# One query tile of two heads in place of two query tiles of one head, in a sparse attention job

## The chip, the cores and the metric

One Trainium2 chip, one of its eight cores. The metric is the device time of one execution in microseconds (us), the median of several runs. A difference of about 0.5% (11 us) is what a measurement of this kernel can tell from no change.

The engines that matter: TensorE multiplies (PE in the profile; PEld is its load of the stationary operand, of which there is one for every matmul), VectorE (DVE) and ScalarE (ACT) do elementwise work, GpSimd (POOL) and SyncE (SP) mostly issue DMAs. In this kernel TensorE's results go to PSUM tiles, which DVE and ACT read.

## The reference

Two layers over a sequence of 1024 tokens. Each has one input projection, two token mixers that read it (stick-breaking attention, 8 heads; native sparse attention, 8 heads in 2 groups of 4, the heads of a group sharing keys and values), gates, two projections that are merged, and an output projection. The sparse part, which is what changes, per query position and head (head size 64):

```
o_cmp: softmax over compressed blocks (up to 63), values vc
sel  : the 8 blocks of 64 keys with the largest group-summed o_cmp probability (some forced)
o_slc: softmax over the keys of the selected blocks, causal,  values vs
o_win: softmax over the last 256 keys,                        values vw
out  = g0 * o_cmp + g1 * o_slc + g2 * o_win        g = sigmoid(gate_logits), per head
b    = out * silu(n_z)
```

All four heads of a group use the same `kc, vc, ks, vs, kw, vw`.

## The kernel before

Everything is f32 in and out. Matmuls run on f32r operands, each value split into a high and a low part: ACT casts the high part out of PSUM, DVE subtracts it to get the low part (`split`, L136 and L137). A product of activations and weights takes three matmuls (L194, L196, L198), an attention product with values two (L917 with the high part, L918 with the low part, in `av`).

A layer runs in stages: `early` (projections for keys, values, queries, gates), `nsa` (sparse attention), `sb` (stick-breaking attention), `output`. In `nsa` and `sb` the attention is cut into jobs, and the rest of the projections is the fill between: `run_jobs` interleaves the scores of the next job (list A) with the products of the current one (list B), and after each step `pump` issues projection matmuls worth a share of the job's planned time (`nsa_us`, four numbers by sequence position m, for four jobs each per group). The framework's scheduler may then move an instruction whose inputs are ready; the order shown further down is the final one.

Before, a sparse job (`head_job`) is one head h over 256 queries: query tiles x = 0 and 1, that is tiles i = 2m and 2m+1 of 128 queries. Scores of tile i span (i+1) x 128 selected keys and min(i+1, 3) x 128 window keys (`nsa_scores`). The exponentials E and ew are scaled by 1/sum and the gate (`nsa_scale`), then turned to keys-by-queries by 128x128 transposes on TensorE (L898), up to four of them in a PSUM tile `tr` (a stage of the `pipeline`, three `tr` buffers), split into `wh` and `wl`, and multiplied with V (`av`). A key tile that both query tiles see gives a matmul of 256 columns. The last key tile is seen by x = 1 alone, and the first of the window by x = 0 alone: those matmuls have 128 columns (`av_stages`, `nsa_av`). The result has the products with V's high part on rows 0 to 63 and low part on 64 to 127; `merge` (L935 on ACT, L936 on DVE) adds them, into the upper or lower half of a 128-row tile by the head's parity, and after two heads `finish_pair` loads the SiLU gate `szl` and multiplies (L926, 128x256).

Of the kernel before, what the change touches and what calls it, by code (L numbers as in the profile page):

```python
# [10 lines left out]
F32 = mybir.dt.float32  # L11
# [4 lines left out]
ALU = mybir.AluOpType  # L16
# [4 lines left out]
P = 128  # L21
S = 1024
# [65 lines left out]
class Trunk:  # L88
    def __init__(self, tc, I, O, depth=2, dbg=None):
        self.tc, self.nc, self.I, self.O, self.depth = tc, tc.nc, I, O, depth  # L90
        self.dbg = dbg or {}
        self.n = 0
        self.fill = []
        self.debt = 0.0
        self.clock, self.seq, self.later = 0.0, 0, []
        self.plan, self.at, self.loaded = [], 0, {}

        self.nsa_us = (1.97, 4.16, 5.85, 7.05)
        self.sb_us = (1.34, 2.87, 4.77, 6.04)
# [12 lines left out]
        self.scb = 2  # L112
        self.adb = 5
# [873 lines left out]
    def nsa(self, l):  # L987
        tc, nc = self.tc, self.nc
        with tc.tile_pool(name=f"nsa{l}", bufs=2, reuse_waits="tile") as pool:
# [9 lines left out]

            def head_job(n, h, st):  # L1000
                g, m = n // 4, n % 4
                hs = {}
                A, B = [], []
                if h == 0:
                    A.append(lambda: load_q(n + 1))
                if m == 3 and h == 3:
                    A.append(lambda: load_kv(g + 1) if g == 0 else self.sb_first())
                for x in range(2):
                    A += self.nsa_scores(pool, g, m, h, x, lambda: qs[n], lambda: kv[g], cmp[n], hs)
                B.append(lambda: self.nsa_scale(pool, g, m, h, hs, cmp[n]))  # L1010
                B += self.nsa_av(pool, g, m, h, lambda: kv[g], cmp[n], hs)

                def fin():
                    if h % 2 == 0:
                        st["o"] = self.tl(pool, [P, 256], F32, "o")
                    self.merge(pool, hs["ps"], st["o"], h % 2)
                    if h % 2 == 1:
                        hd = g * 4 + h - 1
                        self.finish_pair(pool, st["o"], 512 + hd * 64, m, hd * 64)
                B.append(fin)  # L1020
                return A, B, self.nsa_us[m]

            jobs = [cmp_job(0)]
            for n in range(8):
                st = {}
                for h in range(4):
                    if h == 2 and n + 1 < 8:
                        jobs.append(cmp_job(n + 1))
                    jobs.append(head_job(n, h, st))
            self.run_jobs(jobs)  # L1030

    def nsa_cmp(self, pool, g, m, x, q, st):

        nc = self.nc
# [17 lines left out]
        if i == 0:  # L1052
            nc.vector.tensor_tensor(s, s, self.cst("v_cmp").unsqueeze(1).to_broadcast([P, 4, 8]), ALU.mult)
        pg = self.tl(pool, [P, 4, 64], F32, "cpg")
        if nn < 64:
            nc.vector.memset(pg[:, :, nn:64], 0.0)
        gates = self.G[:, i, g * 4:g * 4 + 4]
        if i >= 4:
            nc.vector.tensor_tensor(s, s, rs.unsqueeze(2).to_broadcast([P, 4, nn]), ALU.mult)
            st["sel"][x] = self.nsa_select(pool, i, s, nn)  # L1060
            nc.vector.tensor_tensor(pg[:, :, 0:nn], s, gates.unsqueeze(2).to_broadcast([P, 4, nn]), ALU.mult)
        else:
            gr = self.tl(pool, [P, 4], F32, "cgr")
# [33 lines left out]

    def nsa_scores(self, pool, g, m, h, x, q, kv, cm, hs):

# [7 lines left out]
        def begin():  # L1107
            hs["e", x] = self.tl(pool, [P, S], F32, "E", bufs=4)
            hs["w", x] = self.tl(pool, [P, 384], F32, "ew", bufs=4)
            hs["mx", x] = self.tl(pool, [P, 3], F32, "mx", bufs=4)  # L1110
            if x == 0:
                hs["rs"] = self.tl(pool, [P, 2, 2], F32, "rs")
            return q()[:, h, x * P:x * P + P]

        def row():
            qt = begin()
            ps = self.scores(qt, kv()[0], 0, nk, [])
            nc.vector.tensor_tensor_reduce(hs["e", x][:, 0:nk], ps, self.cst("b_mask")[:, 640 - nk:640], -1.0, 3e38,
                                           ALU.add, ALU.min, hs["mx", x][:, 1:2])

        def half(c):
            qt = begin() if c == 0 else q()[:, h, x * P:x * P + P]
            c1 = min(nk, c * 512 + 512)
            b = c1 - c * 512
            mx = hs["mx", x]
            ps = self.scores(qt, kv()[0], c * 512, c1, [(i * P, "m_causal")] if c == 1 else [])
            bias = cm["sel"][x][:, c * 8:c * 8 + b // 64].unsqueeze(2).to_broadcast([P, b // 64, 64])
            nc.vector.tensor_tensor_reduce(  # L1128
                hs["e", x][:, c * 512:c1].rearrange("p (a b) -> p a b", b=64),
                ps.rearrange("p (a b) -> p a b", b=64), bias, -1.0,  # L1130
                3e38 if c == 0 else mx[:, 0:1], ALU.add, ALU.min, mx[:, c:c + 1])

        def win():
            e, ew, mx, rs = hs["e", x], hs["w", x], hs["mx", x], hs["rs"]
            ps = self.scores(q()[:, h, x * P:x * P + P], kv()[1], k0, nk, [])
# [4 lines left out]
            nc.scalar.activation(e[:, 0:nk], e[:, 0:nk], AF.Exp, bias=mx[:, 1:2], scale=-1.0,  # L1140
                                 accum_out=rs[:, 0, x:x + 1])
            nc.scalar.activation(ew[:, 0:n], ew[:, 0:n], AF.Exp, bias=mx[:, 2:3], scale=-1.0,
                                 accum_out=rs[:, 1, x:x + 1])

        return ([row] if i < 4 else [lambda: half(0), lambda: half(1)]) + [win]

    def nsa_scale(self, pool, g, m, h, hs, cm):

        nc = self.nc
        f = self.tl(pool, [P, 2, 2], F32, "f")  # L1150
        nc.vector.reciprocal(f, hs["rs"])
        gates = self.G[:, 2 * m:2 * m + 2, :].rearrange("p i (b h) -> p b i h", h=8)[:, 1:3, :, g * 4 + h]
        nc.vector.tensor_tensor(f, f, gates, ALU.mult)
        for x in range(2):
            nk = (2 * m + x + 1) * P
            n = min(nk, 384)
            e, ew = hs["e", x], hs["w", x]
            nc.vector.tensor_scalar(e[:, 0:nk], e[:, 0:nk], f[:, 0, x:x + 1], None, ALU.mult)
            nc.scalar.mul(ew[:, 0:n], ew[:, 0:n], f[:, 1, x:x + 1])
        hs["ps"] = self.tl(self.pav, [P, 512], F32, "av", bufs=1)  # L1160

    def nsa_cmp_av(self, g, h, hs, cm):

        c = (h // 2) * 256
        self.av(hs["ps"], [(self.VCS[:, g, h % 2, :], cm["ch"], cm["cl"], (c, c + 256), (0, 256))], False, False)

    def nsa_av(self, pool, g, m, h, kv, cm, hs):
        stages = self.av_stages(pool, m, lambda: (hs["e", 0], hs["e", 1]), lambda: kv()[2])

        def wb(kt, x):  # L1170
            i = 2 * m + x
            k0 = max(0, i - 2)
            return hs["w", x][:, (kt - k0) * P:(kt - k0) * P + P]

        if m > 0:
            a = 2 * m
            stages.append((lambda: [wb(a - 1, 0), wb(a - 1, 1), wb(a, 0), wb(a, 1)],
                           lambda: [(kv()[3][:, a - 1, :], (0, 256), (0, 256)), (kv()[3][:, a, :], (256, 512), (0, 256))]))
            stages.append((lambda: [wb(a - 2, 0), wb(a + 1, 1)],
                           lambda: [(kv()[3][:, a - 2, :], (0, 128), (0, 128)),  # L1180
                                    (kv()[3][:, a + 1, :], (128, 256), (128, 256))]))
        else:
            stages.append((lambda: [wb(0, 0), wb(0, 1), wb(1, 1)],
                           lambda: [(kv()[3][:, 0, :], (0, 256), (0, 256)), (kv()[3][:, 1, :], (256, 384), (128, 256))]))
# [306 lines left out]
```

## Time and profile before

| what | value |
|---|---|
| median of 3 runs | 2206.55 us (2206.5 to 2213.57) |
| the profiled execution | 2207.63 us, its span 2205.8 us (1.8 us lie around it) |
| busy: PE, PEld, DVE, ACT, POOL | 96%, 83%, 72%, 51%, 3% of the span |
| granted TensorE clock, mean over the span | 0.993 |
| `nsa`, layer 0 and 1 | about 297 to 686 us and 1367 to 1757 us |
| `sb`, layer 0 and 1 | about 686 to 954 us and 1757 to 2023 us |

A busy share of PE counts each matmul from its start to its modelled end, and matmuls overlap. How much of the engine one takes is read from start to start in the timeline, not from its duration.

### The profile page before, as it was taken

The numbers are of one execution on the slowest core, as the hardware profiler recorded it, in microseconds if no ns is written. First come the engines' busy times: TensorE is split into PE (matmuls) and PEld (weight loads), VectorE is DVE, ScalarE is ACT, GpSimd is POOL, SyncE is SP. The second block draws the span as 40 slices with busy tenths as digits, with TensorE's granted clock in tenths as the row PEclk, the third lists the DMA queues.
The fourth block names the chain that finished last, engine by engine and source line by source line (L and its number), as shares of the span: only waits on it lengthen the run. The fifth ranks groups of instructions, "written<-read, shape, count | busy, mean of one in ns | idle before, by whom it ended". The sixth has DMA issues, their size and how long they took to land.

```text
span 2205.8 us, 36824 instructions
## 1 busy us (share of the span) xinstructions
PE 2113.4 (96%) x13128; PEld 1831.2 (83%) x13128; DVE 1578.4 (72%) x3722; ACT 1131.5 (51%) x2489; POOL 73.0 (3%) x242
## 2 busy tenths in 40 slices
PE   3999999999999999999999999999999999999999
PEld 3899788988988777779899988889898877777899
DVE  5758568878867778786866863887787587787643
ACT  4433146556666656663533422665666566556410
POOL 2200000000000000000010000000000000001000
PEclk8999999999999999999999999999999999999999
DMA  7546922243225455176456473222522443534433
GB/s 290 108 139 193 303 93 82 91 139 107 78 62 148 125 139 125 64 253 189 151 165 168 129 206 121 92 90 74 149 92 78 124 125 105 148 101 165 152 123 103
DMA packets 254104, 297.05 MB, mean 135 GB/s; under 512 B 38888, under 2 KB 201568, under 8 KB 253920
## 3 DMA queue, kind: packets, MB, share of 16 engines
q1 hardware_dynamic: 213152, 250.65, 37.4%
q10 hardware_dynamic: 36224, 29.37, 5.1%
q0 software_dynamic: 4544, 14.68, 2.4%
q8 instruction: 103, 1.69, 0.3%
q14 instruction: 81, 0.66, 0.1%
HBM read 206.28 MB, written 83.89 MB: 132 GB/s over the span
## 4 chain that ended last, share of the span: by engine, by line
PE 70%; DVE 17%; DMA 5%; issue 3%; ACT 3%; POOL 1%; SPq 1%; DVEq 0%; ACTq 0%; POOLq 0%
PE proj L194 16%; PE proj L198 16%; PE proj L196 16%; PE tr L898 6%; DVE C L1281 4%; PE av L918 4%; PE av L917 3%; PE sc L885 3%; PE sc L886 3%; DVE E L1282 3%; DVE wl L137 2%; DVE w L137 2%; DMA actlo<-AD 1%; DMA ada<-in_ada_w 1%; PE tr L436 1%
## 5 line engine op out<-in xcount | busy, mean ns | idle before, releaser
L194 PE MATMUL proj<-acthi,w 128*128 128x512 f32 x1312 | 537.6, 410 | 3.8 <-ACT acthi L136 1.4
L198 PE MATMUL proj<-acthi,w 128*128 128x512 f32 x1312 | 538.8, 411 | 0.0
L196 PE MATMUL proj<-actlo,w 128*128 128x512 f32 x1312 | 535.1, 408 | 0.5 <-DVE actlo L137 0.5
L136 ACT CAST w<-raw 128x512 fp32r<-128x512 f32 (+1 forms) x296 | 183.2, 622 | 224.0 <-PE proj L198 136.8
L137 DVE TENSOR_TENSOR wl<-tr,wh 128x512 fp32r<-128x512 f32 (+2 forms) x432 | 257.7, 611 | 48.8 <-ACT wh L136 46.1
L194 PEld LDWEIGHTS proj<-acthi,w 128*128 128x128 f32 x1312 | 249.0, 190 | 42.2 <-ACT acthi L136 2.3
L196 PEld LDWEIGHTS proj<-actlo,w 128*128 128x128 f32 x1312 | 248.8, 190 | 36.7 <-DVE actlo L137 1.9
L198 PEld LDWEIGHTS proj<-acthi,w 128*128 128x128 f32 x1312 | 248.5, 189 | 33.9
L137 DVE TENSOR_TENSOR w<-raw,w 128x512 fp32r<-128x512 f32 (+1 forms) x296 | 202.8, 689 | 87.5 <-ACT w L136 84.0
L136 ACT CAST wh<-tr 128x512 fp32r<-128x512 f32 (+2 forms) x432 | 223.0, 527 | 79.9 <-PE tr L898 74.1
L194 PE MATMUL proj<-w,acthi 128*128 128x256 f32 (+1 forms) x768 | 222.3, 290 | 6.8 <-ACT G L813 3.4
L918 PE MATMUL av<-wl,V 128*128 128x256 f32 (+1 forms) x864 | 217.0, 284 | 6.5 <-DVE wl L137 6.5
L198 PE MATMUL proj<-w,actlo 128*128 128x256 f32 (+1 forms) x768 | 221.7, 289 | 0.0
L196 PE MATMUL proj<-w,acthi 128*128 128x256 f32 (+1 forms) x768 | 220.5, 287 | 0.0
L917 PE MATMUL av<-wh,V 128*128 128x256 f32 (+1 forms) x864 | 214.7, 269 | 0.3
L898 PE MATMUL tr<-ident,E 128*128 128x128 f32 x1152 | 187.7, 275 | 22.9 <-DVE E L1282 22.0
L898 PEld LDWEIGHTS tr<-ident,E 128*128 128x128 f32 x1152 | 140.4, 140 | 67.9 <-DVE E L1282 35.2
L1281 DVE TENSOR_TENSOR_SCAN C<-C 128x128 f32<-128x128 f32 (+7 forms) x128 | 173.1, 1352 | 30.7 <-ACT C L1277 29.9
L918 PEld LDWEIGHTS av<-wl,V 128*128 128x128 f32 x864 | 162.7, 188 | 30.1 <-DVE wl L137 17.8
L885 PE MATMUL sc<-kk,q 128*128 128x512 f32 (+3 forms) x512 | 174.4, 341 | 8.0 <-DVE mx L1128 4.3
L886 PE MATMUL sc<-kk,q 128*128 128x512 f32 (+3 forms) x512 | 175.7, 343 | 0.0
L917 PEld LDWEIGHTS av<-wh,V 128*128 128x128 f32 x864 | 163.0, 189 | 10.5 <-ACT wh L136 1.5
(247 smaller groups left out, 3900.1 us busy)
## 6 DMA issues: line engine op xcount, KB each, us to landing
raw<-in_w_in SPq DMA_DIRECT2D x168, 256.0 KB, 3.1
ada<-in_ada_w SPq DMA_DIRECT2D x48, 512.0 KB, 5.5
kk<-QK SPq DMA_DIRECT2D x48, 512.0 KB, 7.4
q<-QK ACTq DMA_DIRECT2D x64, 256.0 KB, 3.9
QK<-s SPq DMA_DIRECT2D x32, 512.0 KB, 2.9
MD<-sz SPq DMA_DIRECT2D x64, 256.0 KB, 2.5
QK<-s SPq DMA_DIRECT2D x48, 256.0 KB, 4.1
VD<-s SPq DMA_DIRECT2D x48, 256.0 KB, 2.0
```

Source lines behind the costliest of these rows:

```text
L136: nc.scalar.copy(hi, src)
L137: nc.vector.tensor_tensor(lo, src, hi.bitcast(F32), ALU.subtract)
L194: nc.tensor.matmul(ps, lh, rh, start=(x == 0), stop=False)
L196: nc.tensor.matmul(ps, lh, rl, start=False, stop=False)
L198: nc.tensor.matmul(ps, ll, rh, start=False, stop=(x == n - 1))
L885: nc.tensor.matmul(ps, q, k[:, 0, c0:c1], start=True, stop=False)
L886: nc.tensor.matmul(ps, q, k[:, 1, c0:c1], start=False, stop=not masks)
L898: nc.tensor.transpose(pt[:, x * P:x * P + P], b, self.ident)
L917: nc.tensor.matmul(ps[:, c:d], lhsT, hi[:, a:b], start=(first and x == 0), stop=False, skip_group_check=True)
L918: nc.tensor.matmul(ps[:, c:d], lhsT, lo[:, a:b], start=False, stop=(last and x == n - 1), skip_group_check=True)
L1281: nc.vector.tensor_tensor_scan(rev, rev, rev, 1.0, ALU.mult, ALU.bypass)
L1282: nc.vector.tensor_tensor(e[:, 0:nk], e[:, 0:nk], c[:, 1:nk + 1], ALU.mult)
```

## The change

A job is now one query tile of 128 queries for two heads of a group (`pair_job`, heads 2hp and 2hp+1 as r = 0, 1). Both heads see the same key tiles, so every product with V has 256 columns: 128 queries of head r = 0, then those of r = 1. A stage is two (key tile, branch) units, four transposes; an odd last unit makes a stage of two. The compressed probabilities are laid out so that the heads of a pair stand side by side too. `merge` and `finish_pair` are replaced by `nsa_merge` and `nsa_finish`: the output tile has 64 rows with the two heads side by side, [64, 2, 256], and the gate load, the multiplication and the store take that shape. `nsa_us` gets eight numbers, one for each tile. The memory set aside for DMA descriptors of GpSimd's queue goes to 8192 bytes.

```
-        self.nsa_us = (1.97, 4.16, 5.85, 7.05)
+        self.nsa_us = (1.5, 2.4, 3.85, 4.5, 5.6, 6.1, 6.85, 7.3)
...
-            def head_job(n, h, st):
+            def pair_job(n, hp, x, st):
...
-                for x in range(2):
-                    A += self.nsa_scores(pool, g, m, h, x, lambda: qs[n], lambda: kv[g], cmp[n], hs)
-                B.append(lambda: self.nsa_scale(pool, g, m, h, hs, cmp[n]))
-                B += self.nsa_av(pool, g, m, h, lambda: kv[g], cmp[n], hs)
+                for r in range(2):
+                    A += self.nsa_scores(pool, g, m, hp * 2 + r, r, x, lambda: qs[n], lambda: kv[g], cmp[n], hs)
+                B.append(lambda: self.nsa_scale(pool, g, m, hp, x, hs))
+                B += self.nsa_av(pool, g, m, hp, x, lambda: kv[g], cmp[n], hs)
...
-                return A, B, self.nsa_us[m]
+                return A, B, self.nsa_us[2 * m + x]
...
+    def nsa_av(self, pool, g, m, hp, x, kv, cm, hs):
+
+        i = 2 * m + x
+        k0 = max(0, i - 2)
+        units = [("e", 2, kt, kt) for kt in range(i + 1)] + [("w", 3, kt, kt - k0) for kt in range(k0, i + 1)]
+        stages = []
+        n = 2 if i else 1
+        for a in range(0, len(units), n):
+            us = units[a:a + n]
+            stages.append((
+                lambda us=us: [hs[w, r][:, c * P:c * P + P] for w, _, _, c in us for r in range(2)],
+                lambda us=us: [(kv()[v][:, kt, :], (y * 256, y * 256 + 256), (0, 256))
+                               for y, (_, v, kt, _) in enumerate(us)]))
         bursts = self.pipeline(pool, stages, lambda: hs["ps"], True)
...
+    def nsa_merge(self, pool, ps, o):
+
+        nc = self.nc
+        t = self.tl(pool, [64, 256], F32, "mt", bufs=1)
+        nc.scalar.copy(t, ps[64:128, 0:256])
+        nc.vector.tensor_tensor(o, ps[0:64, 0:256].rearrange("p (h t) -> p h t", h=2),
+                                t.rearrange("p (h t) -> p h t", h=2), ALU.add)
+
+    def nsa_finish(self, pool, o, hd, m):
+
+        nc = self.nc
+        sz = self.tl(pool, [64, 2, 256], F32, "szl", bufs=1)
+        c = slice(m * 256, m * 256 + 256)
+        r = hd * 64
+        nc.sync.dma_start(sz, self.SZ[r:r + P, c].rearrange("(h d) t -> d h t", d=64))
+        nc.vector.tensor_tensor(o, o, sz, ALU.mult)
+        nc.sync.dma_start(self.AD[512 + r:512 + r + P, c].rearrange("(h d) t -> d h t", d=64), o)
...
-    nc = bacc.Bacc("TRN2", target_bir_lowering=False, num_devices=1)
+    nc = bacc.Bacc("TRN2", target_bir_lowering=False, num_devices=1, dynamic_dma_scratch_size=8192)
```

How TensorE's order changes, at the end of a job of m = 1 in layer 0. Names: `av` is the PSUM accumulator, `wh` and `wl` the split transposes, V_2685 the selected and V_2742 the window values, `ch`, `cl` and VCS the compressed branch, `proj` the fill. Before:

```order
L917 MATMUL av_3862<-wh_3893,V_2685 128x128
L918 MATMUL av_3862<-wl_3894,V_2685 128x128
L917 MATMUL av_3862<-wh_3911,V_2742 128x256
L918 MATMUL av_3862<-wl_3912,V_2742 128x256
L917 MATMUL av_3862<-wh_3911,V_2742 128x256
L918 MATMUL av_3862<-wl_3912,V_2742 128x256
L917 MATMUL av_3862<-ch_3339,VCS_596 128x256
L918 MATMUL av_3862<-cl_3340,VCS_596 128x256
L917 MATMUL av_3862<-wh_3924,V_2742 128x128
L918 MATMUL av_3862<-wl_3925,V_2742 128x128
L917 MATMUL av_3862<-wh_3924,V_2742 128x128
L918 MATMUL av_3862<-wl_3925,V_2742 128x128
```

After, the end of the job of tile i = 2 of one pair of heads:

```order
L917 MATMUL av_3843<-wh_3876,V_2742 128x256
L918 MATMUL av_3843<-wl_3877,V_2742 128x256
L917 MATMUL av_3843<-ch_3335,VCS_596 128x256
L918 MATMUL av_3843<-cl_3336,VCS_596 128x256
L917 MATMUL av_3843<-wh_3893,V_2742 128x256
L198 MATMUL proj_3901<-acthi_28_137,w_3045 128x512
L194 MATMUL proj_3901<-acthi_28_137,w_3050 128x512
L196 MATMUL proj_3901<-actlo_29_138,w_3050 128x512
L885 MATMUL sc_3962<-kk_2609,q_3419 128x128
L918 MATMUL av_3843<-wl_3894,V_2742 128x256
```

The 128-column products are gone, and fill and a score matmul (L885) stand between the last products.

The same on VectorE, at the place where a pair of heads is finished. `E` is the exponential that is scaled by `f`, `sc` the next job's scores. Before:

```order
L1153 TENSOR_TENSOR f_4100<-f_4100,G_594 128x4
L1158 TENSOR_SCALAR E_3973<-E_3973,f_4100 128x640
L137 TENSOR_TENSOR s_766_4062<-proj_3919,s_766_4062 128x512
L1158 TENSOR_SCALAR E_4024<-E_4024,f_4100 128x768
L936 TENSOR_TENSOR o_3952<-av_3971,mt_4080 64x256
L926 TENSOR_TENSOR o_3952<-o_3952,szl_4083 128x256
L1128 ISA E_4091,mx_4093<-sc_4095,irep_3654 128x512
```

After:

```order
L1161 TENSOR_TENSOR f_4070<-f_4070,G_594 128x4
L1196 TENSOR_TENSOR o_3921<-av_3940,mt_4049 64x2x128
L1166 TENSOR_SCALAR E_3942<-E_3942,f_4070 128x640
L1206 TENSOR_TENSOR o_3921<-o_3921,szl_4052 64x512
L1134 ISA E_4060,mx_4062<-sc_4064,irep_3678 128x512
L1134 ISA mx_4062 128x1
L1166 TENSOR_SCALAR E_3995<-E_3995,f_4070 128x640
```

The finishing multiplication is 512 wide on 64 rows instead of 256 wide on 128, and here it stands ahead of the second scaling, which the next transposes read.

## Rows read from the trace of the kernel before

**Rows 1.** Busy time by engine (us, with counts) in the two `nsa` stages.
```profile
core 0: us, PE busy (x) PEld busy (x) DVE busy (x) ACT busy (x) POOL busy (x), PEclk, DMA share, GB/s
297.00:686.00 389.00, 383.32 (x2490) 336.05 (x2491) 297.05 (x930) 242.55 (x587) 1.74 (x11) 1.00 0.32 97
...
1367.00:1757.00 390.00, 384.36 (x2504) 337.13 (x2502) 299.36 (x934) 244.72 (x590) 1.88 (x11) 1.00 0.33 100
```

**Rows 2.** Waits of PE and PEld, 297 to 686: us in total, times, longest.
```profile
PE sc L885 <- DVE mx L1128: 2.2, 3, 1.5
...
PEld sc L885 <- DVE mx L1118: 4.0, 8, 1.0
...
PEld tr L898 <- DVE wl L137: 2.7, 6, 0.7
PEld av L918 <- DVE wl L137: 2.0, 7, 0.4
```

**Rows 3.** Products with V by shape, 297 to 686: busy us, mean ns | idle.
```profile
L918 PE MATMUL av<-wl,V 128*128 128x256 f32 x184 | 48.9, 284 | 0.0
...
L918 PE MATMUL av<-wl,V 128*128 128x128 f32 x88 | 23.0, 275 | 0.0
...
L917 PE MATMUL av<-wh,V 128*128 128x128 f32 x88 | 19.6, 237 | 0.0
```

**Rows 4.** PE's timeline, four products of 128 columns: start us, duration us.
```profile
385.70 0.22 PE L917 MATMUL av<-wh,V 128*128 128x128 f32 x1
385.76 0.28 PE L918 MATMUL av<-wl,V 128*128 128x128 f32 x1
385.88 0.27 PE L917 MATMUL av<-wh,V 128*128 128x128 f32 x1
385.99 0.27 PE L918 MATMUL av<-wl,V 128*128 128x128 f32 x1
386.10 0.45 PE L194 MATMUL proj<-acthi,w 128*128 128x512 f32 x1
386.39 0.39 PE L196 MATMUL proj<-actlo,w 128*128 128x512 f32 x1
386.62 0.39 PE L198 MATMUL proj<-acthi,w 128*128 128x512 f32 x1
```

**Rows 5.** PE's timeline, two of 256 columns, two of 128, then fill.
```profile
415.87 0.28 PE L917 MATMUL av<-wh,V 128*128 128x256 f32 x1
415.99 0.28 PE L918 MATMUL av<-wl,V 128*128 128x256 f32 x1
416.11 0.22 PE L917 MATMUL av<-wh,V 128*128 128x128 f32 x1
416.17 0.28 PE L918 MATMUL av<-wl,V 128*128 128x128 f32 x1
416.28 0.33 PE L196 MATMUL proj<-w,acthi 128*128 128x256 f32 x1
416.45 0.28 PE L198 MATMUL proj<-w,actlo 128*128 128x256 f32 x1
```

**Rows 6.** DVE by shape, 297 to 686: the low parts and the finish.
```profile
L137 DVE TENSOR_TENSOR wl<-tr,wh 128x512 fp32r<-128x512 f32 x72 | 49.0, 687 | 9.7 <-ACT wh L136 9.3
...
L137 DVE TENSOR_TENSOR wl<-tr,wh 128x384 fp32r<-128x384 f32 x40 | 21.7, 552 | 1.8 <-ACT wh L136 1.4
...
L137 DVE TENSOR_TENSOR wl<-tr,wh 128x256 fp32r<-128x256 f32 x24 | 10.0, 417 | 1.7 <-ACT wh L136 1.7
L926 DVE TENSOR_TENSOR o<-o,szl 128x256 f32<-128x256 f32 x16 | 6.8, 422 | 0.2
```

**Rows 7.** DVE by shape, whole span: a 512-wide product of two SBUF tiles.
```profile
L1446 DVE TENSOR_TENSOR gt<-gt,gt 128x512 f32<-128x512 f32 x32 | 22.0, 689 | 0.5
```

**Rows 8.** Instructions on the tile `szl`: what ended DVE's wait (us, times), landing of its load.
```profile
  DMA szl<-SZ: 0.9, 1
...
DMA to landing us min/median/max: 2.3/2.7/4.9
```

**Rows 9.** DMA issues by line: queue, count, KB each, median us to landing.
```profile
q<-QK ACTq DMA_DIRECT2D x64, 256.0 KB, 3.9
...
actlo<-AD POOLq DMA_DIRECT2D x4, 1024.0 KB, 7.5
```

More of the change, by code (lines that the diff above doesn't have):

```diff
@@ L1003, in head_job @@
                 A, B = [], []
-                if h == 0:
+                if hp == 0 and x == 0:
                     A.append(lambda: load_q(n + 1))
-                if m == 3 and h == 3:
+                if m == 3 and hp == 1 and x == 1:
                     A.append(lambda: load_kv(g + 1) if g == 0 else self.sb_first())
-                for x in range(2):
-                    A += self.nsa_scores(pool, g, m, h, x, lambda: qs[n], lambda: kv[g], cmp[n], hs)
-                B.append(lambda: self.nsa_scale(pool, g, m, h, hs, cmp[n]))
-                B += self.nsa_av(pool, g, m, h, lambda: kv[g], cmp[n], hs)
+                for r in range(2):
+                    A += self.nsa_scores(pool, g, m, hp * 2 + r, r, x, lambda: qs[n], lambda: kv[g], cmp[n], hs)
+                B.append(lambda: self.nsa_scale(pool, g, m, hp, x, hs))
+                B += self.nsa_av(pool, g, m, hp, x, lambda: kv[g], cmp[n], hs)
                 def fin():
[L1014 to L1019, printed above, removed]
+                    if x == 0:
+                        st["o"] = self.tl(pool, [64, 2, 256], F32, "o")
+                    self.nsa_merge(pool, hs["ps"], st["o"][:, :, x * P:x * P + P])
+                    if x == 1:
+                        self.nsa_finish(pool, st["o"], g * 4 + hp * 2, m)
                 B.append(fin)
-                return A, B, self.nsa_us[m]
+                return A, B, self.nsa_us[2 * m + x]
             jobs = [cmp_job(0)]
             for n in range(8):
[L1025 to L1029, printed above, removed]
+                for hp in range(2):
+                    st = {}
+                    for x in range(2):
+                        if hp == 1 and x == 0 and n + 1 < 8:
+                            jobs.append(cmp_job(n + 1))
+                        jobs.append(pair_job(n, hp, x, st))
             self.run_jobs(jobs)
@@ L1053, in nsa_cmp, with wide @@
             nc.vector.tensor_tensor(s, s, self.cst("v_cmp").unsqueeze(1).to_broadcast([P, 4, 8]), ALU.mult)
-        pg = self.tl(pool, [P, 4, 64], F32, "cpg")
+        pg = self.tl(pool, [P, 2, 2, 64], F32, "cpg")
         if nn < 64:
-            nc.vector.memset(pg[:, :, nn:64], 0.0)
+            nc.vector.memset(pg[:, :, :, nn:64], 0.0)
+        pr = pg.rearrange("p r h n -> p h r n")[:, :, :, 0:nn]
+        sr = s.rearrange("p (h r) n -> p h r n", r=2)
+        def wide(f):
+            return f.rearrange("p (h r) -> p h r", r=2).unsqueeze(3).to_broadcast([P, 2, 2, nn])
         gates = self.G[:, i, g * 4:g * 4 + 4]
@@ L1060, in nsa_cmp @@
             st["sel"][x] = self.nsa_select(pool, i, s, nn)
-            nc.vector.tensor_tensor(pg[:, :, 0:nn], s, gates.unsqueeze(2).to_broadcast([P, 4, nn]), ALU.mult)
+            nc.vector.tensor_tensor(pr, sr, wide(gates), ALU.mult)
         else:
@@ L1064, in nsa_cmp @@
             nc.vector.tensor_tensor(gr, rs, gates, ALU.mult)
-            nc.vector.tensor_tensor(pg[:, :, 0:nn], s, gr.unsqueeze(2).to_broadcast([P, 4, nn]), ALU.mult)
+            nc.vector.tensor_tensor(pr, sr, wide(gr), ALU.mult)
         st["pg"][x] = pg
@@ L1070, in nsa_cmp_t @@
         for x in range(2):
-            for hp in range(2):
-                self.nc.tensor.transpose(pt[:, hp * 256 + x * P:hp * 256 + x * P + P],
-                                         st["pg"][x][:, hp * 2:hp * 2 + 2].rearrange("p a b -> p (a b)"), self.ident)
+            for r in range(2):
+                self.nc.tensor.transpose(pt[:, x * 256 + r * P:x * 256 + r * P + P],
+                                         st["pg"][x][:, r].rearrange("p a b -> p (a b)"), self.ident)
         st["ch"] = self.tl(pool, [P, 512], F32R, "ch")
@@ L1096, in nsa_select, with nsa_scores @@
         return rep
-    def nsa_scores(self, pool, g, m, h, x, q, kv, cm, hs):
+    def nsa_scores(self, pool, g, m, h, r, x, q, kv, cm, hs):
         nc = self.nc
@@ L1107, in begin @@
         def begin():
[L1108 to L1111, printed above, removed]
+            hs["e", r] = self.tl(pool, [P, S], F32, "E", bufs=4)
+            hs["w", r] = self.tl(pool, [P, 384], F32, "ew", bufs=4)
+            hs["mx", r] = self.tl(pool, [P, 3], F32, "mx", bufs=4)
+            if r == 0:
                 hs["rs"] = self.tl(pool, [P, 2, 2], F32, "rs")
@@ L1117, in row @@
             ps = self.scores(qt, kv()[0], 0, nk, [])
-            nc.vector.tensor_tensor_reduce(hs["e", x][:, 0:nk], ps, self.cst("b_mask")[:, 640 - nk:640], -1.0, 3e38,
-                                           ALU.add, ALU.min, hs["mx", x][:, 1:2])
+            nc.vector.tensor_tensor_reduce(hs["e", r][:, 0:nk], ps, self.cst("b_mask")[:, 640 - nk:640], -1.0, 3e38,
+                                           ALU.add, ALU.min, hs["mx", r][:, 1:2])
         def half(c):
@@ L1124, in half @@
             b = c1 - c * 512
-            mx = hs["mx", x]
+            mx = hs["mx", r]
             ps = self.scores(qt, kv()[0], c * 512, c1, [(i * P, "m_causal")] if c == 1 else [])
@@ L1128, in half @@
             nc.vector.tensor_tensor_reduce(
-                hs["e", x][:, c * 512:c1].rearrange("p (a b) -> p a b", b=64),
+                hs["e", r][:, c * 512:c1].rearrange("p (a b) -> p a b", b=64),
                 ps.rearrange("p (a b) -> p a b", b=64), bias, -1.0,
@@ L1133, in win @@
         def win():
-            e, ew, mx, rs = hs["e", x], hs["w", x], hs["mx", x], hs["rs"]
+            e, ew, mx, rs = hs["e", r], hs["w", r], hs["mx", r], hs["rs"]
             ps = self.scores(q()[:, h, x * P:x * P + P], kv()[1], k0, nk, [])
@@ L1140, in win, with nsa_scale @@
             nc.scalar.activation(e[:, 0:nk], e[:, 0:nk], AF.Exp, bias=mx[:, 1:2], scale=-1.0,
-                                 accum_out=rs[:, 0, x:x + 1])
+                                 accum_out=rs[:, 0, r:r + 1])
             nc.scalar.activation(ew[:, 0:n], ew[:, 0:n], AF.Exp, bias=mx[:, 2:3], scale=-1.0,
-                                 accum_out=rs[:, 1, x:x + 1])
+                                 accum_out=rs[:, 1, r:r + 1])
         return ([row] if i < 4 else [lambda: half(0), lambda: half(1)]) + [win]
-    def nsa_scale(self, pool, g, m, h, hs, cm):
+    def nsa_scale(self, pool, g, m, hp, x, hs):
@@ L1149, in nsa_scale @@
         nc = self.nc
+        i = 2 * m + x
         f = self.tl(pool, [P, 2, 2], F32, "f")
         nc.vector.reciprocal(f, hs["rs"])
-        gates = self.G[:, 2 * m:2 * m + 2, :].rearrange("p i (b h) -> p b i h", h=8)[:, 1:3, :, g * 4 + h]
+        h0 = g * 4 + hp * 2
+        gates = self.G[:, i, :].rearrange("p (b h) -> p b h", h=8)[:, 1:3, h0:h0 + 2]
         nc.vector.tensor_tensor(f, f, gates, ALU.mult)
[L1154 to L1159, printed above, removed]
@@ L1160, in nsa_scale @@
-        hs["ps"] = self.tl(self.pav, [P, 512], F32, "av", bufs=1)
[L1162 to L1184, printed above, removed]
-        bursts = self.pipeline(pool, stages, lambda: hs["ps"], True)
-        return bursts[:-1] + [lambda: (self.nsa_cmp_av(g, h, hs, cm), bursts[-1]())]
@@ new lines, in nsa_scale, with nsa_cmp_av @@
+        nk = (i + 1) * P
+        n = min(nk, 384)
+        for r in range(2):
+            e, ew = hs["e", r], hs["w", r]
+            nc.vector.tensor_scalar(e[:, 0:nk], e[:, 0:nk], f[:, 0, r:r + 1], None, ALU.mult)
+            nc.scalar.mul(ew[:, 0:n], ew[:, 0:n], f[:, 1, r:r + 1])
+        hs["ps"] = self.tl(self.pav, [P, 512], F32, "av", bufs=1)
+    def nsa_cmp_av(self, g, hp, x, hs, cm):
+        c = x * 256
+        self.av(hs["ps"], [(self.VCS[:, g, hp, :], cm["ch"], cm["cl"], (c, c + 256), (0, 256))], False, False)
@@ new lines, in nsa_av @@
+    def nsa_av(self, pool, g, m, hp, x, kv, cm, hs):
+        i = 2 * m + x
+        k0 = max(0, i - 2)
[8 more added lines that the diff above has]
+                               for y, (_, v, kt, _) in enumerate(us)]))
+        bursts = self.pipeline(pool, stages, lambda: hs["ps"], True)
+        return bursts[:-1] + [lambda: (self.nsa_cmp_av(g, hp, x, hs, cm), bursts[-1]())]
```

## The prediction

> **What bounds the kernel now.** I read the busy time by stage first, because the change touches only the two `nsa` stages. In 389 us of layer 0 PE is busy for 383.3 us, DVE for 297.1 and ACT for 242.6; layer 1 is the same within 1 us, at a granted clock of 1.00 in both [rows 1]. Then the waits: what PE or its weight load waits for is nearly always DVE, either a score buffer that DVE has to read (2.2 us and 4.0 us for the largest entries) or the low part of a split (2.7 and 2.0 us) [rows 2]. Each is small against 389 us. So PE is the bound in these stages, DVE is next (76% of the time, 92 us idle per layer), and ACT is far off. Whatever shortens PE's own stream shortens the stage, as long as DVE keeps up. The durations of PE's instructions don't tell what they cost, since they overlap: a product of 128 columns lasts 237 or 275 ns, one of 256 columns 284 [rows 3]. For the cost I read the timeline from start to start [rows 4, 5].
>
> **The products with V.** Before, a job of m = 0 has four matmuls of 128 columns (two in its selected, two in its window part), a job of m = 1 to 3 has six (two and four). Per layer there are 8 jobs of the first kind and 24 of the second: 32 + 144 = 176, 88 on each of the two lines [rows 3]. After, none is left: there are 88 matmuls of 256 columns for them, with as many columns in sum. All other products keep their number and shape.
>
> What do 128 columns cost? In a run of four, the first start is followed by the next after 0.06 us, the others after 0.12, 0.11 and 0.11, and the 512-column matmul behind them takes 0.29 us to the next start, where the one after it takes 0.23. From the first of the four to the end of that stretch is 386.39 - 385.70 = 0.69 us, less 0.23 for the 512 columns: 0.46 us for four [rows 4]. In a run of two, 416.45 - 416.11 = 0.34 us, less 0.12 for the 256-column matmul behind it: 0.22 us for two. The two 256-column products ahead of them take 0.12 us each [rows 5]. So a product costs 0.11 us with 128 columns and 0.12 us with 256: half the columns save next to nothing, and what the first seems to save (0.06) the matmul behind the run pays back.
>
> Per layer that is 24 runs of four at 0.46 and 40 runs of two at 0.22, 11.0 + 8.8 = 19.8 us before, and 88 x 0.12 = 10.6 us after: 9.2 us less, 18.4 us in both layers. Bounds: nothing, if columns alone counted; 40 us by the durations, (88 x (237 + 275) - 88 x 284) ns = 20.1 us per layer [rows 3]. I take 18.4, since it comes from starts in the place itself.
>
> The Trainium skill speaks against this gain: "TensorE: Matmul & The Clock Gate", section "Back-to-back issue gap", gives an isolated gap of columns / 2.4 + 2.5 ns at full clock, 56 ns for 128 columns and 109 for 256. An estimate from it is 176 x 0.056 - 88 x 0.109, some 0.3 us per layer, nothing. The trace agrees with it for 256 columns (0.12 us) and not for 128 (0.11 us on average). The same page, section "LDWEIGHTS (loading the stationary operand)", puts a load of 128 columns at 128 / 1.2 = 107 ns, which would be the floor that the 128-column rows show; an estimate with it is 9.2 us per layer.
>
> **DVE.** The finish of a pair goes from 256 to 512 elements on each row, on half the rows. A 256-wide product takes 422 ns [rows 6], a 512-wide one 689 [rows 7]: 16 x 0.267 = 4.3 us more per layer. Against it, the stages are fewer. Before: 72 of 512 columns, 40 of 384, 24 of 256, in sum 49.5 + 22.1 + 10.0 = 81.6 us for the low parts [rows 6]. After: a tile i has (i + 1) + min(i + 1, 3) units, two to a stage, which gives 104 stages of 512 columns and 20 of 256 per layer, 71.4 + 8.3 = 79.8 us. Net on DVE: +2.5 us per layer, +5.0 in all. DVE has 92 us of idle time per layer to hide this in, but PE's waits are waits for DVE [rows 2], and the order puts the longer finish ahead of a scaling that the next transposes read. So I charge the whole 5.0 us to the path. Its bounds are -3.6 us (the finish hidden, the shorter splits felt) and +8.6 us (the reverse). ACT gets the same twelve casts fewer per layer and is not the bound: nothing.
>
> **What I cost at nothing.** Transposes (456 per layer), scores, exponentials, scalings and merges keep their number and their elements. The planned fill of `nsa` is 8 x (1.97 + 4.16 + 5.85 + 7.05) = 152.2 us per layer before and 4 x 38.1 = 152.4 after, so `sb` inherits the same rest. The loads of `szl` and the stores keep bytes and 1 KB rows, in 64 partitions instead of 128. DVE waited for such a load once, 0.9 us, and it lands in 2.7 us (4.9 at most) [rows 8], with most of a pair's time between its issue and its use. The nearest load into 64-row pieces, q with twice the bytes, lands in 3.9 [rows 9]. If that cover were gone, 32 finishes x 1.2 us = 38 us; with one wait in 64 I take nothing. SP's queue has the store behind the finish, so weight loads behind it go out 0.27 us later, well inside their lead. The smaller descriptor memory touches only GpSimd's loads. A load of 1 MB there lands in 7.5 us [rows 9]; if the queue had to pause once per layer that is at most 15 us. POOL's instructions stand in the same order, and I take nothing.
>
> **The sum.** 2207.6 us (the profiled execution, 1.8 above its span) - 18.4 + 5.0 = 2194.2. The median of the runs lies 1.1 below that execution: 2193 us, 0.6% faster. The forecast's own range is 2187 to 2200, by the bounds on DVE (5.0 against -3.6 and 8.6) and a few us for another interleaving of fill.
>
> **Rivals.** *DVE becomes the bound in m = 0 to 2*, so PE's gain there turns into longer waits, and only m = 3 keeps its own: 16 jobs x (0.46 + 0.22 - 3 x 0.12) = 5.1 us, about 2201. For it: all the larger waits are for DVE [rows 2], and its work grows. Against: 92 us idle per layer. Chance 0.12.
>
> *Columns alone count*, so PE gains nothing and DVE's 5 us are felt: 2207.6 + 5.0 - 1.1 = 2211, no change. That is the Trainium skill's gap rule as a mechanism. For it: the 0.06 us after the first product of each run. Against: every other start in rows 4 and 5. Chance 0.08.
>
> *Waits go too.* A job of m = 1 has four stages for three `tr` buffers, and the fourth waits for DVE's split (2.7 us among PEld's waits); tile i = 2 has three stages. If PE's own idle time (389 - 383.3 = 5.7 us per layer) vanished, 2193 - 11 = 2182. Against: i = 3 to 7 have four to six stages. Chance 0.07.
>
> *Slower: the products come too soon after their transposes.* Between the two lie the cast on ACT and the subtraction on DVE (687 ns for 512 columns), and nearly all stages are now 512 wide, where 64 of 136 were narrower. PEld's waits for low parts, 2.7 + 2.0 us [rows 2], are 35 ns per stage. With 248 stages in both layers the net gain of 13.4 us is gone at 54 ns more per stage, and 100 ns more is slower by over 0.5%; at four times today's wait (105 ns more) the time is 2193 + 26 = 2219. For it: in the changed order, products still follow a burst of a dozen transposes after one or two fill matmuls. Against: so they do before. Chance 0.11.
>
> **How the numbers follow.** The forecast gets 0.62. By the bound of 0.5% (some 11 us), faster is below 2195.5 and slower above 2217.6. Of the forecast's range some four fifths lie below 2195.5 in weight, since I charged DVE in full: 0.48 faster, 0.14 same. With the vanishing waits faster is 0.55; with the two middle rivals same is 0.34; slower is 0.11. The range reaches from the faster rival, 2182, to just past the gap rule's, 2212.
>
> **What would show it.** Right: no L917 or L918 of 128 columns left in `nsa`, each `nsa` stage 5 to 8 us shorter, `sb` unchanged, DVE's finish at 0.69 us, and PE's and PEld's waits for `wl` no larger than before. Wrong: `nsa` keeps its 389 us although the 128-column products are gone. If then the waits for `wl`, `mx` or E have grown by 6 us or more per layer, DVE or the lead was mis-sized; if the waits are the same and the remaining products start further apart, the spacing was. A finish that waits for `szl`, or a longer `output` stage, would show a cost that I put at nothing.

## The result and the profile after

The changed kernel takes 2184.47 us, the median of four runs (2181.0 to 2188.37), against 2209.31 us before in the same comparison: ratio 0.9895, 95% interval 0.988 to 0.9909, some 25 us or 1.1% faster. The forecast was 2193 with a range of 2182 to 2212: right in sign, and short by 9 us. The time lies below the forecast's own range (2187 to 2200), and inside the whole one only because that was drawn down to 2182 for the rival in which waits go too. A second comparison (e5 below) gave 2183.28, 24.5 us less than before there, and a ratio of 0.9885 (0.9868 to 0.9901).

Where it came from is read by stage first. The stage `nsa` is taken here from its first compressed score to the end of its last finish, in each kernel. Before, busy time of each engine (columns as in [rows 1]):

```profile
289.90:684.30 394.40, 388.72 (x2523) 340.99 (x2522) 299.65 (x935) 243.81 (x588) 1.74 (x11) 0.99 0.32 97
1367.10:1754.50 387.40, 381.75 (x2491) 335.00 (x2490) 298.63 (x932) 243.77 (x588) 1.78 (x10) 1.00 0.33 99
sum 781.80, PE 770.48 PEld 675.99 DVE 598.29 ACT 487.58 POOL 3.53; mean PE 385.24 PEld 338.00 DVE 299.14 ACT 243.79 POOL 1.76
```

After:

```profile
296.80:677.50 380.70, 378.26 (x2436) 333.15 (x2435) 297.81 (x923) 242.85 (x576) 1.74 (x11) 0.99 0.35 101
1361.90:1735.70 373.80, 371.78 (x2404) 326.57 (x2403) 296.89 (x920) 242.27 (x576) 1.41 (x10) 1.00 0.36 103
sum 754.50, PE 750.04 PEld 659.72 DVE 594.71 ACT 485.12 POOL 3.15; mean PE 375.02 PEld 329.86 DVE 297.35 ACT 242.56 POOL 1.58
```

The stages are 13.7 and 13.6 us shorter, 27.3 us together, where the prediction had 5 to 8 us each. That is a little more than the whole gain of 25 us. It has two parts. PE's busy time falls by 20.4 us, and its idle time (stage less busy) from 11.3 to 4.5 us, 6.9 less.

Some of the gain is lost between the layers. From the end of the last finish of `sb` in layer 0 to `nsa` of layer 1, before and then after:

```profile
952.30:1367.10 414.80, 409.52 (x2602) 365.88 (x2601) 272.15 (x651) 157.90 (x299) 16.16 (x26) 1.00 0.57 170
945.10:1361.90 416.80, 410.87 (x2607) 366.75 (x2605) 272.52 (x651) 159.02 (x301) 15.90 (x26) 1.00 0.57 169
```

This stretch takes 414.8 to 415.2 us in the three profiles of the old jobs and 416.2 us or more in all of the new ones. The prediction had no such cost, and its cause is open.

DVE, which I charged with 5 us more, is busy for 3.6 us less. That is not less work: added one by one, the durations of its instructions in the two stages are 697.1 us before and 701.1 after (698.5 in e5, the same kernel once more), 1.4 to 4.0 us more. Busy time counts overlapping records once, and after the change more of DVE's instructions start before the one ahead has ended (1362 against 1274). In this execution `nsa` of layer 0 starts 7 us later than before (296.8 against 289.9); in all other profiles of the changed jobs it starts at 288 to 292 us, so this belongs to the one execution. Part of it is the clock: in this execution the granted clock was 0.50 from 253.4 to 260.2 us, where it was 1.00 before.

The products with V in `nsa` of layer 0, and DVE's low parts and finish there (shape, count | busy us, mean ns | idle), to be held against [rows 3, 6]:

```profile
L917 PE MATMUL av<-wh,V 128*128 128x256 f32 x228 | 61.0, 284 | 0.1
L918 PE MATMUL av<-wl,V 128*128 128x256 f32 x228 | 60.6, 287 | 0.0
```

```profile
L137 DVE TENSOR_TENSOR wl<-tr,wh 128x512 fp32r<-128x512 f32 x104 | 70.1, 687 | 10.6 <-ACT wh L136 10.3
...
L1206 DVE TENSOR_TENSOR o<-o,szl 64x512 f32<-64x512 f32 x16 | 10.9, 681 | 0.2
L137 DVE TENSOR_TENSOR wl<-tr,wh 128x256 fp32r<-128x256 f32 x20 | 8.1, 418 | 1.2 <-ACT wh L136 1.2
```

No product of 128 columns is left; per layer, 88 of 256 came for 176 of 128. The finish takes 681 ns where 689 were assumed, the stages are 104 and 20. What PE's weight load waits for, in the same stage (us, times, longest), against [rows 2]:

```profile
PEld sc L885 <- DVE mx L1143: 2.3, 6, 0.9
PEld tr L898 <- DVE E L1166: 1.5, 6, 0.3
PEld av L917 <- ACT wh L136: 1.4, 4, 0.5
...
PEld tr L898 <- DVE wl L137: 0.7, 2, 0.5
...
PEld av L918 <- DVE wl L137: 0.5, 2, 0.3
```

The largest entry of the score matmul has gone from 4.0 us to 2.3, the transposes' wait for a split from 2.7 to 0.7, and the products' for a low part from 2.0 to 0.5; their wait for a high part has grown from 0.8 to 1.4.

PE's own waits say which of these made it idle. `mx` is what DVE writes as it reads a score buffer. Before, beside the 2.2 us in [rows 2]:

```profile
PE sc L885 <- DVE mx L1118: 1.9, 3, 0.7
```

After:

```profile
PE tr L898 <- DVE ib L1094: 0.7, 1, 0.7
PE sc L885 <- DVE mx L1143: 0.7, 2, 0.5
PE sc L885 <- DVE mx L1134: 0.4, 1, 0.4
```

A score matmul that waits for DVE to read a score buffer cost PE 4.1 of its 5.7 us of idle time in layer 0 before, and 1.1 us after. So both the spacing and the waits moved. The experiments ask how much belongs to the width of the products, and how much to the jobs' new shape, their plan or the finish.

### The profile page after: what moved, and what is told of

Its sections match the earlier page's. It is cut to its first block, busy times and chain, and to the rows that moved or that the text cites. A ratio compares the mean times of both kernels' runs of the same rounds, so it can differ in the third digit from the quotient of the medians.

```text
span 2186.6 us, 36378 instructions
## 1 busy us (share of the span) xinstructions
PE 2096.8 (96%) x12952; PEld 1817.6 (83%) x12952; DVE 1575.6 (72%) x3698; ACT 1130.8 (52%) x2465; POOL 72.4 (3%) x242
## 4 chain that ended last, share of the span: by engine, by line
PE 72%; DVE 15%; DMA 4%; issue 4%; ACT 3%; POOL 1%; SPq 0%; DVEq 0%; ACTq 0%; POOLq 0%
PE proj L194 16%; PE proj L198 16%; PE proj L196 16%; PE tr L898 6%; DVE C L1302 5%; PE av L918 4%; PE av L917 3%; PE sc L885 3%; PE sc L886 3%; DVE E L1303 3%; DVE wl L137 2%; DVE w L137 1%; ACT wh L136 1%; DMA ada<-in_ada_w 1%; DMA actlo<-AD 1%
## 5 line engine op out<-in xcount | busy, mean ns | idle before, releaser
L918 PE MATMUL av<-wl,V 128*128 128x256 f32 (+1 forms) x776 | 202.1, 287 | 5.5 <-DVE wl L137 5.5
L917 PE MATMUL av<-wh,V 128*128 128x256 f32 (+1 forms) x776 | 202.0, 278 | 0.4 <-ACT E L1146 0.2
L885 PE MATMUL sc<-kk,q 128*128 128x512 f32 (+3 forms) x512 | 174.2, 340 | 2.1 <-DVE mx L1143 0.9
L918 PEld LDWEIGHTS av<-wl,V 128*128 128x128 f32 x776 | 146.0, 188 | 25.7 <-DVE wl L137 13.0
L917 PEld LDWEIGHTS av<-wh,V 128*128 128x128 f32 x776 | 146.4, 189 | 13.7 <-ACT wh L136 3.2
```

The source lines that it names most:

```text
L885: nc.tensor.matmul(ps, q, k[:, 0, c0:c1], start=True, stop=False)
L917: nc.tensor.matmul(ps[:, c:d], lhsT, hi[:, a:b], start=(first and x == 0), stop=False, skip_group_check=True)
L918: nc.tensor.matmul(ps[:, c:d], lhsT, lo[:, a:b], start=False, stop=(last and x == n - 1), skip_group_check=True)
```

## Experiments

**Products of 128 columns made 256 wide in the kernel before.** Nothing else is edited; jobs, stages, plan and finish are those of before.

```
-        stages = self.av_stages(pool, m, lambda: (hs["e", 0], hs["e", 1]), lambda: kv()[2])
+        stages = self.av_stages(pool, m, lambda: (hs["e", 0], hs["e", 1]), lambda: kv()[2], True)
...
-                           lambda: [(kv()[3][:, a - 2, :], (0, 128), (0, 128)),
-                                    (kv()[3][:, a + 1, :], (128, 256), (128, 256))]))
+                           lambda: [(kv()[3][:, a - 2, :], (0, 256), (0, 256)),
+                                    (kv()[3][:, a + 1, :], (0, 256), (0, 256))]))
...
-                                 (v()[:, 2 * a + 1, :], (256, 384), (128, 256))]))
+                                 (v()[:, 2 * a + 1, :], *(((128, 384), (0, 256)) if wide else ((256, 384), (128, 256))))]))
```

The window part of m = 0 is widened in the same way.

> The kernel before, but each of the 352 products with V that had 128 columns in nsa takes 256 (columns that belong to another product; the result is no longer the reference's). Theory A, a product of 128 columns already costs what one of 256 does (0.11 against 0.12 us): 352 x 0.01 = at most 3.5 us more, 2209 to 2213 us, and the nsa stages stay within 2 us of before. Rival B, only columns count (0.056 against 0.109 us): 352 x 0.053 = 18.7 us more, about 2228, and the gain of the change comes from shorter waits alone.

Measured: 2203.41 us, ratio to before 0.9981 (0.9972 to 0.999). With twice the columns in 352 products the kernel is 4 us faster, which neither theory had. Its timeline, four of the widened products and the fill behind them (start, duration), beside [rows 4]:

```profile
347.61 0.28 PE L917 MATMUL av<-wh,V 128*128 128x256 f32 x1
347.73 0.28 PE L918 MATMUL av<-wl,V 128*128 128x256 f32 x1
347.85 0.28 PE L917 MATMUL av<-wh,V 128*128 128x256 f32 x1
347.97 0.28 PE L918 MATMUL av<-wl,V 128*128 128x256 f32 x1
348.09 0.40 PE L196 MATMUL proj<-actlo,w 128*128 128x512 f32 x1
348.32 0.39 PE L198 MATMUL proj<-acthi,w 128*128 128x512 f32 x1
```

From the first product to the second fill matmul it is 0.71 us, with 128 columns it was 0.69 [rows 4]. So width costs almost nothing, as theory A has it. The 4 us are in the waits; the sums over both `nsa` stages:

```profile
sum 776.30, PE 771.27 PEld 677.72 DVE 595.09 ACT 486.67 POOL 3.53; mean PE 385.63 PEld 338.86 DVE 297.54 ACT 243.33 POOL 1.76
```

PE is busy 0.8 us longer than before and idle for 5.0 us instead of 11.3. Its waits for a score buffer in layer 0, 4.1 us before, come down to one:

```profile
PE sc L885 <- DVE mx L1128: 0.8, 1, 0.8
```

TensorE's order is not the same: the scheduler places transposes, scores and fill otherwise around 256-column products, and in layer 0 about a tenth of TensorE's instructions stand elsewhere.

**Products of the changed kernel cut in two.** The reverse: as many 128-column products as before, in the new jobs.

```
+        cut = lambda w, kt: (kt == i) if i % 2 else (w == "w" and i > 0 and kt == k0)
...
-                lambda us=us: [(kv()[v][:, kt, :], (y * 256, y * 256 + 256), (0, 256))
-                               for y, (_, v, kt, _) in enumerate(us)]))
+                lambda us=us: [(kv()[v][:, kt, :], (y * 256 + c, y * 256 + d), (c, d))
+                               for y, (w, v, kt, _) in enumerate(us)
+                               for c, d in (((0, 128), (128, 256)) if cut(w, kt) else ((0, 256),))]))
```

> The changed kernel, but 88 products of 256 columns per layer are each cut into two of 128, so that it has as many 128-column products as before; the result stays the same. Theory A: the cut gives back 18.4 us, 2203 us, and 6 us of the measured gain of 25 remain for shorter waits. Rival B (only columns count): no change, 2184 to 2186.

Measured: 2211.91 us, ratio 1.0018 (1.0009 to 1.0028): the whole gain is gone, and a little more. B is refuted. A's size is not met either: 27 to 29 us came back and not 18.4.

```profile
sum 781.80, PE 768.98 PEld 676.33 DVE 600.87 ACT 487.36 POOL 3.15; mean PE 384.49 PEld 338.17 DVE 300.44 ACT 243.68 POOL 1.57
```

Against the changed kernel `nsa` is 27.3 us longer, of which PE is busy for 18.9 and idle for 8.4 (12.8 against 4.5). Its waits for a score buffer in layer 0 are back, 4.1 us with the smallest entry:

```profile
PE sc L885 <- DVE mx L1134: 2.1, 2, 1.5
PE sc L885 <- DVE mx L1124: 1.8, 3, 0.8
```

So the jobs' new shape, the eight planned times and the finish together are worth nothing beyond the width of the products.

**Half of the finish.**

```
-        nc.vector.tensor_tensor(o, o, sz, ALU.mult)
+        nc.vector.tensor_tensor(o[:, 0], o[:, 0], sz[:, 0], ALU.mult)
```

> The changed kernel, but the finish of a pair multiplies one of the two heads by its gate only, 256 elements on a row instead of 512; the other head's gate is left out. As I predicted, the longer finish is on the path: 32 x 0.267 = 8.5 us less, 2176. If DVE's idle time hides it: within 2 us of the changed kernel, 2183 to 2186.

Measured: 2182.53 us, ratio 0.9886 (0.9873 to 0.9898), within 2 us of the changed kernel. DVE's busy time falls by 6.6 us over both stages (588.08 against 594.71), and the stages don't get shorter (755.0 against 754.5):

```profile
sum 755.00, PE 749.04 PEld 658.29 DVE 588.08 ACT 485.05 POOL 3.15; mean PE 374.52 PEld 329.14 DVE 294.04 ACT 242.52 POOL 1.57
```

DVE's idle time hides the finish. My charge of 5 us was wrong.

**Four planned times instead of eight, twice, and the changed kernel again.**

```
-        self.nsa_us = (1.5, 2.4, 3.85, 4.5, 5.6, 6.1, 6.85, 7.3)
+        self.nsa_us = (1.97, 1.97, 4.16, 4.16, 5.85, 5.85, 7.05, 7.05)
```

> The changed kernel with the four planned times of before, each for both tiles of its m: (1.97, 1.97, 4.16, 4.16, 5.85, 5.85, 7.05, 7.05). If the 6 us beyond the spacing of products come from fill that is planned per tile: about 2190. If they come from the shape of the jobs (stages of four transposes, fewer of them): within 2 us of the changed kernel.

> The changed kernel once more, beside the next three on one chip, since its profile began nsa 7 us later than all others while nsa itself was as short as in e4. If that was this one execution: nsa of layer 0 starts at 288 to 292 us, and the time is 2180 to 2186 us.

> The kernel of e4 (four planned times instead of eight) once more. If the plan is worth the 5.6 us that lay between the medians: 5 us below e5 again. If that was the spread between executions (its two nsa stages were only 1.2 us shorter in sum): within 2 us of e5.

Measured: e4 2178.86, ratio 0.987 (0.9856 to 0.9884); e5 2183.28, 0.9885 (0.9868 to 0.9901); e6 2179.46, 0.9871 (0.9856 to 0.9886). In e5 `nsa` starts at 290.4 us, so the late start was one execution's. The flat plan is 3.8 us below the changed kernel in e6 (against e5, in one comparison) and 5.6 in e4 (against the first result, in another). Its stages in e6 are 3.3 us shorter in sum than those of e5 (755.3):

```profile
sum 752.00, PE 748.12 PEld 658.60 DVE 595.04 ACT 484.11 POOL 3.14; mean PE 374.06 PEld 329.30 DVE 297.52 ACT 242.06 POOL 1.57
```

So the plan per tile earns nothing of the gain; if anything it costs some 4 us. The intervals of e5 and e6 overlap, so this is likely, not settled. It is the fastest version I have.

**The cut with TensorE's order held.** `nsa` is run with TensorE's order as written (`tc.manual_schedule(engines={mybir.EngineType.PE})` around `run_jobs`), once as the change has it and once with the cut of e2. TensorE's order of the two is the same row by row but for the cut; DVE's and ACT's still differ in a few places.

> The changed kernel with TensorE's order in nsa as the program writes it, not moved by the scheduler. It is the base for e8. Theory A1, the scheduler's order is worth little: 2180 to 2190 us. Rival: waits grow without it, above 2195.

> e7 with the cut of e2 (88 products of 256 columns per layer as two of 128 each), and TensorE's order otherwise the same row by row. e2 gave back 27 us where the spacing alone says 18.4. Theory A1, the rest of 9 us came from another order that the scheduler chose for 128-column products: here e7 + 17 to 20 us. Theory A2, a 128-column product costs more than its spacing shows, whatever the order: e7 + 25 to 29 us. Rival B, columns alone count: e7 + 2 at most.

Measured: 2253.55 and 2269.14 us, 15.6 us apart, a little under what A1 gives and far from A2 and B. The scheduler's order turns out to be worth 70 us. Sums over the two stages, e7 then e8:

```profile
sum 823.60, PE 766.82 PEld 664.79 DVE 603.94 ACT 490.71 POOL 3.14; mean PE 383.41 PEld 332.40 DVE 301.97 ACT 245.36 POOL 1.57
```

```profile
sum 838.30, PE 784.80 PEld 684.03 DVE 606.54 ACT 489.88 POOL 3.14; mean PE 392.40 PEld 342.01 DVE 303.27 ACT 244.94 POOL 1.57
```

PE's busy time grows by 18.0 us, the 18.4 of the prediction. Its idle time does not grow, as in e2, but falls by 3.3 (56.8 to 53.5). With the order held, the cut adds no waits. (In e8's stages the granted clock was 0.50 for 3.4 us more than in e7's, which can make up to 1.7 of the 18.0 us.) A reservation: e7 has 57 us of idle time, in which some waits may be lost, so this shows the cost of the cut more surely than where the other waits come from.

**Spacing by width, alone.** Behind the end of the changed kernel:

```
...
+                for cols in (64, 128, 192, 256, 384, 512):
+                    for k in range(64):
+                        nc.tensor.matmul(ps[:, :cols], hi[:, k % 8, k // 16 * P:k // 16 * P + P], lo[:, k % 8, :cols],
+                                         start=(k == 0), stop=(k == 63))
```

> The changed kernel with 64 products each of 64, 128, 192, 256, 384 and 512 columns behind its end, one after another into one accumulator that nothing reads, each with its own 128-column stationary operand; only their spacing counts. Theory A: 64, 128 and 192 columns all go at about 0.11 us, 256 at 0.11 to 0.12, 384 at 0.17, 512 at 0.23. Rival B, columns alone: 0.03, 0.056, 0.08, 0.11, 0.16, 0.22. Theory A2 (128 columns cost more than their spacing in the kernel): 0.13 or more at 128.

The stretches of 64, 128, 192 and 256 columns (stretch, its us, PE busy with the instructions that touch it, PEld, granted clock, DMA):

```profile
2177.60:2183.40 5.80, 5.80 (x53) 5.80 (x54) 1.00 0.07 23
2185.80:2199.10 13.30, 13.30 (x64) 13.30 (x64) 0.50 0.00 0
2204.20:2208.60 4.40, 4.40 (x42) 4.40 (x41) 1.00 0.02 4
2208.80:2216.30 7.50, 7.50 (x65) 7.50 (x64) 1.00 0.00 0
```

At the full granted clock (2.4 GHz) 64 columns go at 0.11 us and 192 at 0.11; 256 at 0.12. The two widths cost the same: there is a floor under the spacing. The 128-column stretch itself fell into a granted clock of 0.50 (1.2 GHz), at 0.21 us each, so its value at full clock is shown only by its neighbours and by [rows 4, 5].

The trace of the kernel before has the floor too, further down in width. Its products of one column (L373), 16 at a granted clock of 1.00 and 8 at 0.50, from the first start to the last end:

```profile
31.60 1.84 PE L373 MATMUL av<-ones,acc 128*128 128x1 f32 x16
41.15 1.84 PE L373 MATMUL tr<-ones,acc 128*128 128x1 f32 x8 [7.71 <-DVE acc L481]
```

From start to start these are 0.11 and 0.21 us.

**As many stages as before.** The last two units of tiles 2, 4 and 6 get a stage each, 136 stages a layer.

```
+        cuts = list(range(0, len(units), n))
+        if i in (2, 4, 6):
+            cuts.append(len(units) - 1)
...
```

> The changed kernel with as many stages as before, 136 a layer and not 124: the last two units of tiles 2, 4 and 6 get a stage each. Products and transposes are the same. If the fewer stages carry the gain beyond the spacing: 4 to 9 us above e5, 2187 to 2192. If it is the 128-column products that spoil the order, as e1 and e2 suggest: within 2 us of e5, 2181 to 2185.

Measured: 2182.75 us, ratio 0.9887 (0.9872 to 0.9902), as e5. The number of stages and the casts saved carry nothing.

**The smaller descriptor memory alone, in the kernel before** (`dynamic_dma_scratch_size=8192`).

> The kernel before with the smaller descriptor memory alone. I costed it at nothing: 2205 to 2212. At most one landing per layer more in the output stage: 2222.

Measured: 2207.19 us, ratio 1.0002 (0.9992 to 1.0011): nothing.

**Fill moved from `nsa` to `sb`**, on top of the flat plan.

```
-        self.nsa_us = (1.97, 1.97, 4.16, 4.16, 5.85, 5.85, 7.05, 7.05)
-        self.sb_us = (1.34, 2.87, 4.77, 6.04)
+        self.nsa_us = (1.8, 1.8, 3.9, 3.9, 5.5, 5.5, 6.6, 6.6)
+        self.sb_us = (1.44, 3.1, 5.17, 6.53)
```

> e6 with 9.8 us per layer of planned fill moved from nsa to sb (nsa 1.8, 3.9, 5.5, 6.6 for both tiles; sb 1.44, 3.1, 5.17, 6.53). nsa has almost no PE waits left, sb has some 14 us per layer, most of them for the exponential that DVE scales. If more fill covers them: 5 to 15 us below e6, 2165 to 2175. If sb's waits are DVE's own pace: 2178 to 2182.

Measured: 2180.8 us, 0.9879 (0.9863 to 0.9896). A miss for the first reading. `nsa` is 20.2 us shorter than in e6 (731.8 against 752.0) and `sb` 16.1 us longer (550.5 against 534.4). The moved fill did find idle time in `sb`: PE's fell there from 29.2 to 24.6 us. But the stretch between the layers is 5.6 us longer (422.0 against 416.4), and nothing is left. Why, and whether the two belong together, is open.

## Why the prediction was right, and where it fell short

- *The products with V, 18.4 us.* Right, in mechanism and size. PE's busy time fell by 20.4 us; the cut alone changes it by 18.9 (e2) and by 18.0 with the order held (e8 against e7). The rival that columns alone count is refuted by e1, e2 and e8.
- *The Trainium skill, "TensorE: Matmul & The Clock Gate".* The isolated gap of the section "Back-to-back issue gap" is not the spacing here: 56 ns against 0.11 us at 128 columns, 109 ns against 0.12 us at 256. The same section says that at small widths this gap counts too little, since it leaves out the weight load, so the prediction took it for more than it is. The 107 ns of the section "LDWEIGHTS (loading the stationary operand)" lie close to the floor of 0.11 us that the runs show from 1 to 192 columns. That it is the load which makes the floor is an argument and not shown: in the traces the records of these loads last 0.19 us, longer than the spacing.
- *DVE, 5.0 us charged in full.* This step failed. Its sizes were about right (681 ns for the finish, 1.4 to 4.0 us more work in all), its place was not: e3 takes 6.6 us of DVE's busy time away and the stages stay. The idle time per layer hid it, as the text itself allowed with its bound of -3.6.
- *Waits, taken as unchanged.* The second miss: PE's idle time fell by 6.9 us. The rival "waits go too" had a bound for it (11 us) but a wrong cause, the number of stages per job, and wrong waits, those for a split; e10 brings the stages back and the time stays, and what shrank is mostly the wait for a score buffer. The waits go with the width of the products: e1 removes 6.3 us of idle time with nothing but wider products in the old jobs, e2 brings 8.4 back with narrower ones in the new jobs, and with the order held the cut brings none. This points to the order that the scheduler makes around 128-column products as the cause. It is likely and not settled, by the reservation on e7; why the order is worse for them was not looked into.
- *Costed at nothing.* The descriptor memory: right (e11). The plan of fill: nearly; eight times for four cost some 4 us, if anything. The load of `szl` lands in 3.2 us where it took 2.7, and DVE never waits for it. `sb` takes as long as before (535.2 us in both layers, 535.1 before). The stretch between the layers does not: it is 2 us longer, a cost that the prediction lacks.
- *The slower rival*, products too soon after their transposes: refuted. The waits for low parts fell.

With the two misses put right, 18.4 + 6.9 = 25.3 us, against 25 measured. That fit is closer than the account: the stages alone gave 27.3, and the rest of the kernel took some back. That the time lies in the stated range is in part luck. Both misses have the same sign and put it 2.5 us below the forecast's own range, and the bound that still holds it (2182) was set by a rival whose cause was not the one at work.

## What to carry to other kernels

Count what an instruction takes from start to start, up to the start of the second one behind the run: a short matmul that seems cheap there may be paid back by its neighbour, and below some width (at 192 columns and fewer here) narrower is no cheaper, so two narrow products that can become one wide one can be worth the regrouping. Where a scheduler places instructions, a change of width also changes the order, and the waits with it; test that part by holding the order or by changing the width alone. Do not charge a longer instruction to the path because its engine is the one waited for; a shorter one in its place costs one run and tells.

## What the runs showed of the hardware that was not expected

The floor under the spacing goes with TensorE's granted clock. In e9 it was 0.11 us at 1.00 (64 and 192 columns) and 0.21 us at 0.50 (128 columns); the products of one column in the kernel before show the same two values. The granted clock fell to 0.50 while PE was busy without a pause, 6 us into a stream of 64-column products behind 256-column ones, and rose to 1.00 again in the stream of 192-column products:

```profile
2165.00:2177.50 12.50, 12.50 (x109) 12.50 (x108) 3.40 (x8) 0.00 (x0) 0.00 (x0) 1.00 0.30 96
2177.60:2185.60 8.00, 8.00 (x66) 8.00 (x64) 0.85 (x2) 0.00 (x0) 0.00 (x0) 0.87 0.06 18
2185.70:2199.30 13.60, 13.60 (x65) 13.60 (x66) 0.00 (x0) 0.00 (x0) 0.00 (x0) 0.50 0.00 0
2199.40:2208.70 9.30, 9.30 (x65) 9.30 (x65) 0.00 (x0) 0.00 (x0) 0.00 (x0) 0.75 0.01 2
2208.80:2216.40 7.60, 7.60 (x66) 7.60 (x65) 0.00 (x0) 0.00 (x0) 0.00 (x0) 1.00 0.00 0
```

PE is busy for the whole of each of these stretches. The same happened in the kernel before: in the stream of one-column products at 292.0 to 297.0 us the granted clock fell from 1.00 to 0.50, with PE busy throughout. In `nsa` itself the granted clock was 0.99 to 1.00 before and after, with 6.8 us at 0.50 in each, so it plays no part in the gain of the stages.
